# More expert groups made ahead, scatter-adds in eights between the row gathers, and row dots inside two top-k passes

## The chip, the cores and the metric

The kernel runs on one core of a Trainium2 chip. The metric is the device time of one execution in microseconds (us). The core has five engines with a fixed instruction order each: TensorE (PE, matmuls), VectorE (DVE), ScalarE (ACT), GpSimd (POOL) and SyncE (SP, which only issues DMAs). Each executes its own list in order and waits, where needed, for semaphores of the others or of DMAs. The lists are fixed when the kernel is built.

## The reference

The model is a two-layer trunk over 512 tokens of width 1024 in float32. Each layer is a mixer (pooling and retention, or a gated recurrence), then PEER, a layer of 16,384 single-row experts of which every token uses 8 heads x 16. PEER is where the change lies:

```python
q = (xt @ w_q).reshape(T, HEADS, 2, 128)
s = einsum('thpd,hpkd->thpk', q, sub_keys)          # 8 heads x 2 halves x 128 keys
s_top, i_top = top_k(s, 16)
cand = s_top[:, :, 0, :, None] + s_top[:, :, 1, None, :]
best, pos = top_k(cand.reshape(T, HEADS, 256), 16)
eid = take_along_axis(cand_id, pos); gate = softmax(best)
act = gelu(einsum('td,thkd->thk', xt, u_tab[eid]))
out = einsum('thk,thkd->td', gate * act, v_tab[eid])
```

A residual with layer norm follows each half.

## The kernel before

Tokens stand in four blocks (tb) of 128. Experts stand in 128 blocks of 128, four blocks to a group, 32 groups. Matmuls in float32 are made from three products of parts: a weight piece of 128 x 1024 is loaded by SP (`stream`, L173), ACT casts its high half `hi` (L169), DVE subtracts to get the low half `lo` (L170), and PE runs hi x hi, lo x hi and hi x lo (L185 to L187).

Most tokens use the experts densely: `mm1` makes the activations of one expert block for 352 tokens (24 matmuls of 352 columns), and the expert stage multiplies them by gates and by v. Block 3's 128 tokens gather their rows one by one in the expert stage (L968 to L993). The first 32 tokens of block 0 take a third way, the class `Scatter`: `place` (L79) gathers their u rows (POOL, L741), `dots` (L105, DVE) forms their dot products, `weigh` applies the Gelu (ACT, L111) and multiplies it into the gates (DVE, L113), and `add` (L127, POOL) adds the gates of block 0 to a table `gz` in HBM by indirect DMAs, 16 to a head, 128 to a layer. A head's adds wait until all of the previous head have landed.

The order in one PEER layer is as follows.

1. `route_topk`, four chunks c. A chunk projects a quarter of wq on PE (`proj_T`, 96 matmuls of 512 columns, which need four weight pieces, called a to d below). For each token block the keys are multiplied (L851) and DVE takes the top 16 of four key rows (L860 to L864). For block 0, `choose` then selects the experts of the chunk's two heads and `place` issues eight gathers of u rows into four buffers, `urow` and `urow3`. So the fifth gather needs the first four dots done. Before the change, dots stand behind token blocks 2 and 3, four each, then weigh, and the adds of a head stand behind it or behind the next chunk's choose. The next chunk's projection runs on PE while DVE still works on token blocks 2 and 3, and its weight halves are subtracted on DVE among the top-k.
2. `choose` for token blocks 3, 1 and 2, with PE transposes (L834).
3. `route_gates`, eight slices of 32 tokens, each in quarters: DVE makes one-hot tiles `oh`, `og` (L900, L901), PE multiplies them (L910, L911), ACT writes `gbuf` (L912), SP writes the slice to `gd` in HBM (L916).
4. `experts`: the expert blocks in turn, with 18 matmuls of 512 columns each (L1096), reading gates back from gd and gz.

Steps 1 to 3 leave PE room, so `lookahead` (L757) makes activations ahead: `NLA` groups of four mm1 blocks. They are placed by credits: the generators of steps 1 to 3 yield a cost at certain points, and each 2.8 credits puts one mm1 block there. What is left is made behind the last gate slice. The groups made ahead are written to HBM (`sp`, 704 KB a group) and read back in step 4, but for the last two (`KEEP`). The other groups' mm1 blocks are made in step 4, four blocks ahead of their use.

Of the kernel before, what the change touches and what calls it, by code (L numbers as in the profile page):

```python
# [15 lines left out]
ALU = mybir.AluOpType  # L16
# [16 lines left out]
NU = 32  # L33
TN = TD - NU
US = NU // 32
QN = P // NU
QC = 32 // QN
GQ = 8
LAG = GQ + 4
NSD = TD // 32  # L40
NLA = 19
NSZ = 4
KEEP = 2
ROT = 3
RAW = 5
QS = 8
Y2 = 1.85
YC = (1.5, 3.0, 3.0, 4.0)
AHEAD = 4
TAIL = 4  # L50
# [5 lines left out]
LANDED = mybir.DependencyInfo(mybir.DependencyClass.Sync, mybir.DependencyReason.DATA)  # L56


class Scatter:


    def __init__(self, k, pool, layer):
        nc, self.tc = k.nc, k.tc
        self.name = "gz%d" % layer
        self.layer = layer
        self.last = []
        self.todo = []
        self.gate = [k.pe.tile([P, 2, 16], F32, name="gate0", tag="gate0", bufs=4) for _ in range(4)]
        self.idx = [k.pe.tile([P, 2 * 16], I32, name="idx0", tag="idx0", bufs=4) for _ in range(4)]
        self.pcol = pool.tile([P, 1], F32, name="pcol", tag="pcol")  # L70
        nc.sync.dma_start(out=self.pcol, in_=k.io["pcol"])
        self.dst = k.dram.tile([NG, P, NSZ, NB, 32], F32, name=self.name, tag=self.name)
        z = pool.tile([P, NSZ * NB * 32], F32, name="zero", tag="zero")
        nc.gpsimd.memset(z, 0.0)
        for g in range(NG):
            nc.sync.dma_start(out=self.dst[g].rearrange("p s b t -> p (s b t)"), in_=z)

    def place(self, k, pool, c, k0, k1):
        nc = k.nc  # L79
        idx = self.idx[c]  # L80
        x = pool.tile([P, P], F32, name="ix0", tag="fi")[:, :32]
        y = pool.tile([P, P], F32, name="iy0", tag="fj")[:, :32]
        e = pool.tile([P, 32], I32, name="eu", tag="eu")
        ids = pool.tile([P, QC], I32, name="ids", tag="ids", bufs=2)
        nc.vector.scalar_tensor_tensor(e[:NU], k0[:NU], 128.0, k1[:NU], ALU.mult, ALU.add)
        for q in range(QN):
            nc.scalar.copy(ids[q * NU:(q + 1) * NU], e[:NU, q * QC:(q + 1) * QC])  # L87
        self.rows = []
        for j in range(QC):
            r, self.fetch = k.urow(pool, self.layer, ids, j)  # L90
            self.rows.append((j, r))
# [15 lines left out]
    def weigh(self, k, pool):  # L107
        nc = k.nc
        act = pool.tile([P, 32], F32, name="actu", tag="actu")
        for q in range(QN):  # L110
            nc.scalar.activation(act[:NU, q * QC:(q + 1) * QC], self.av[q * NU:(q + 1) * NU], AF.Gelu)  # L111
        gate = self.gate[self.chunk].rearrange("p h s -> p (h s)")
        nc.vector.tensor_tensor(gate[:NU], gate[:NU], act[:NU], ALU.mult)  # L113
        self.todo += [self.chunk * 2, self.chunk * 2 + 1]

    def add(self, k, n=1):
        nc, tc = k.nc, k.tc
        flat = self.dst.rearrange("g p s b (t o) -> (g p s b t) o", o=1)
        for _ in range(min(n, len(self.todo))):
            hd = self.todo.pop(0)  # L120
            c, h = divmod(hd, 2)
            gate = self.gate[c].rearrange("p h s -> p (h s)")
            key = "%s.%d" % (self.name, hd)
            head = []
            with tc.issue_after(self.fetch):
                for j in range(h * 16, h * 16 + 16):
                    d = nc.gpsimd.indirect_dma_start(  # L127
                        out=flat, out_offset=bass.IndirectOffsetOnAxis(ap=self.idx[c][:, j:j + 1], axis=0),
                        in_=gate[:, j:j + 1], in_offset=None, compute_op=ALU.add).ins
                    for p in self.last:  # L130
                        tc.add_manual_dep(d, p.name, LANDED, reason="adds of different heads may meet")
                    tc.declare_no_dep(d, group=key, reason="a head's sixteen experts differ")
                    tc.add_to_no_dep_group(key, d)
                    head.append(d)
            self.last = head

    def read(self, engine, out, g):
        d = engine.dma_start(out=out, in_=self.dst[g]).ins
        for p in self.last:
            self.tc.add_manual_dep(d, p.name, LANDED, reason="all adds of the last head")  # L140


class Kern:
# [623 lines left out]
    def route_topk(self, layer, xT, kT, gz):  # L767
        nc, tc, io = self.nc, self.tc, self.io
        with tc.tile_pool(name="rt", bufs=1) as rt, tc.tile_pool(name="rt2", bufs=2) as rt2, \
# [14 lines left out]
            def choose(tb, h0, n):  # L784
# [14 lines left out]
                for h in range(n):  # L799
                    c2 = rs2.tile([P, 64], F32, name="c2", tag="c2")  # L800
                    cv = cand[:, h, :]
                    nc.vector.max(out=best[:, h, 0:8], in_=cv)
                    nc.vector.max_index(out=pos[:, h, 0:8], in_max=best[:, h, 0:8], in_values=cv)
                    nc.vector.match_replace(out=c2, in_to_replace=best[:, h, 0:8], in_values=cv, imm_value=NEG)
                    nc.vector.max(out=best[:, h, 8:16], in_=c2)
                    nc.vector.max_index(out=pos[:, h, 8:16], in_max=best[:, h, 8:16], in_values=c2)
                    yield 0.7
                if tb == 3:
                    gate = self.gate3.rearrange("p (h s) -> p h s", h=8)
                elif tb == 0:  # L810
                    gate = gz.gate[h0 // 2]
# [30 lines left out]
            for c in range(4):  # L842
# [4 lines left out]
                for tb in range(NTB):  # L847
# [4 lines left out]
                                         start=True, stop=True)  # L852
                    ixs = rs2.tile([P, 4, 16], U32, name="ix", tag="ix", bufs=2)
                    for i in range(4):
                        hp = c * 4 + i
                        sc = ps[:, i * P:(i + 1) * P]
                        mx = stop[:, tb, hp, :]
# [371 lines left out]
```

## Time and profile before

| | |
|---|---|
| Median of three runs | 2801.23 us (2800.25 to 2803.93) |
| The profiled execution's own time | 2803.68 us |
| Its span on the core | 2801.9 us |
| Busy time of PE, DVE, POOL, ACT | 2745.8, 2359.3, 1352.6, 1116.5 us |
| Bytes moved | 788.34 MB |
| POOL adds (L127) | 256, 486.2 us busy |
| POOL gathers of u rows (L741) | 64, 86.9 us busy |

A row of a timeline reads: start in us, duration in us, engine, line, operation, output tile <- input tiles, shape, and in brackets the time the engine had idled before, with what ended that idle. A row of the waits reads: engine, tile and line that waited, engine, tile and line waited for, total us, times, longest. In the windows, PE busy etc. are us with the number of instructions, PEclk is the granted clock of TensorE as a share of full speed, DMA the busy share of its engines. "ACT ch" is a cast gate product ahead of an expert matmul, "DVE ka" and "kb" are tiles of the choose stage.

### The profile page before, as it was taken

What the parts mean: (1) busy time and instruction counts of PE and PEld (TensorE: products, weight loads), DVE (VectorE), ACT (ScalarE), POOL (GpSimd) and SP (SyncE); (2) the same over time, 40 slices, a digit from 0 to 9 for tenths busy, and PEclk for the clock granted to TensorE, in tenths of its full rate; (3) what the DMA queues carried; (4) which work ended last, traced back from release to release, by engine and by line L of the source; (5) the groups of instructions that cost most, each with busy time, mean ns of one, the idle gap of its engine ahead of it and who ended that gap; (6) DMA issues with size and microseconds to landing.
All of it is one profiled execution on the core that took longest, in us unless ns stands there. A gap on an engine that the chain in (4) does not pass through costs nothing.

```text
span 2801.9 us, 41670 instructions
## 1 busy us (share of the span) xinstructions
PE 2745.8 (98%) x15314; PEld 2449.4 (87%) x15314; DVE 2359.3 (84%) x4556; ACT 1116.5 (40%) x1575; POOL 1352.6 (48%) x865
## 2 busy tenths in 40 slices
PE   9999999999999999999999999999989999999998
PEld 7899899988888888888788898999978888888886
DVE  6678989867898989888798677899868888988887
ACT  3353336543333333333334343445543333333332
POOL 0006667864565666553000017667764556555651
PEclk9999999999999999999999999999999999999999
DMA  6357776999999999998222557686999999999993
GB/s 228 127 178 227 236 221 178 248 270 366 382 386 382 390 377 396 374 383 295 95 83 72 203 177 203 194 245 177 277 308 361 378 398 368 389 388 382 384 383 146
DMA packets 318318, 788.34 MB, mean 281 GB/s; under 512 B 62113, under 2 KB 128161, under 8 KB 318113
## 3 DMA queue, kind: packets, MB, share of 16 engines
q1 hardware_dynamic: 175808, 410.75, 41.4%
q0 software_dynamic: 120128, 303.22, 32.0%
q10 hardware_dynamic: 22176, 71.71, 6.4%
q8 instruction: 120, 1.97, 0.3%
q14 instruction: 86, 0.70, 0.1%
HBM read 708.50 MB, written 77.07 MB: 280 GB/s over the span
## 4 chain that ended last, share of the span: by engine, by line
PE 86%; DVE 7%; DMA 3%; POOL 2%; issue 1%; ACT 1%; SPq 0%; DVEq 0%; POOLq 0%; ACTq 0%
PE pB L1096 18%; PE pC L1096 18%; PE pA L187 12%; PE pA L185 12%; PE pA L186 12%; PE pC L185 2%; PE pC L186 2%; PE pC L187 2%; POOL gz L127 2%; DMA urow<-in_u,ids 2%; DVE lo L170 1%; PE pB L910 1%; DMA gd<-gbuf 1%; PE pB L911 1%; PE pB L851 1%
## 5 line engine op out<-in xcount | busy, mean ns | idle before, releaser
L169 ACT CAST hi<-raw 128x1024 fp32r<-128x1024 f32 (+1 forms) x609 | 637.8, 1050 | 962.9 <-PE pC L1096 368.2
L170 DVE TENSOR_TENSOR lo<-raw,hi 128x1024 fp32r<-128x1024 f32 (+1 forms) x609 | 733.7, 1215 | 184.5 <-ACT hi L169 156.4
L187 PE MATMUL pA<-xThi,lo 128*128 128x352 f32 (+2 forms) x1872 | 628.7, 336 | 11.2 <-DVE lo L170 11.2
L185 PE MATMUL pA<-xThi,hi 128*128 128x352 f32 (+2 forms) x1872 | 631.2, 337 | 0.6 <-ACT hi L169 0.3
L968 POOL DMA_INDIRECT row<-in_u,eid x256 | 407.3, 1591 | 464.4 <-DVE av L980 369.2
L186 PE MATMUL pA<-xTlo,hi 128*128 128x352 f32 (+2 forms) x1872 | 627.4, 335 | 0.6 <-DVE xTlo L170 0.6
L127 POOL DMA_INDIRECT gz<-gate,idx x256 | 486.2, 1899 | 130.6 <-issue 84.2
L968 POOL DMA_INDIRECT row<-in_v,eid x256 | 361.9, 1414 | 145.1 <-issue 58.5
L187 PEld LDWEIGHTS pA<-xThi,lo 128*128 128x128 f32 x1872 | 353.7, 189 | 28.6 <-DVE lo L170 14.1
L185 PEld LDWEIGHTS pA<-xThi,hi 128*128 128x128 f32 x1872 | 354.0, 189 | 18.3 <-ACT hi L169 1.2
L186 PEld LDWEIGHTS pA<-xTlo,hi 128*128 128x128 f32 x1872 | 353.9, 189 | 17.3 <-DVE xTlo L170 1.2
L993 DVE SCALAR_TENSOR_TENSOR h<-row,cf,h 128x1024 f32<-128x1024 f32 x256 | 329.4, 1287 | 6.7 <-DMA row<-in_v,eid 6.4
L980 DVE CUSTOM_DVE_ANT_0 row<-row,x 128x1024 f32<-128x1024 f32 x256 | 311.6, 1219 | 10.0 <-DMA row<-in_u,eid 9.7
L1096 PE MATMUL pB<-hi,ch 128*128 128x512 f32 x768 | 300.2, 391 | 17.9 <-DMA raw<-in_peer_ut 9.7
L1096 PE MATMUL pC<-hi,ch 128*128 128x512 f32 x768 | 299.9, 390 | 0.0
L1096 PE MATMUL pC<-lo,ch 128*128 128x512 f32 x768 | 299.6, 390 | 0.0
L1096 PE MATMUL pB<-hi,cl 128*128 128x512 f32 x768 | 299.6, 390 | 0.0
L1096 PE MATMUL pB<-lo,ch 128*128 128x512 f32 x768 | 299.5, 390 | 0.0
L1096 PE MATMUL pC<-hi,cl 128*128 128x512 f32 x768 | 299.3, 390 | 0.0
L170 DVE TENSOR_TENSOR cl<-gt,ch 128x768 fp32r<-128x768 f32 x128 | 122.0, 953 | 117.0 <-ACT ch L169 117.0
L741 POOL DMA_INDIRECT urow<-in_u,ids x64 | 86.9, 1358 | 273.4 <-ACT ids L87 203.7
L169 ACT CAST ch<-gt 128x768 fp32r<-128x768 f32 x128 | 107.2, 837 | 249.4 <-PE pC L1096 152.2
(280 smaller groups left out, 4541.9 us busy)
## 6 DMA issues: line engine op xcount, KB each, us to landing
raw<-in_peer_ut SPq DMA_DIRECT2D x256, 512.0 KB
raw<-in_peer_v SPq DMA_DIRECT2D x256, 512.0 KB
gd<-gbuf SPq DMA_DIRECT2D x16, 2048.0 KB
gt<-gd ACTq DMA_DIRECT2D x60, 512.0 KB
sp<-ge SPq DMA_DIRECT2D x34, 704.0 KB
ge<-sp ACTq DMA_DIRECT2D x34, 704.0 KB
raw<-in_peer_w_q SPq DMA_DIRECT2D x32, 512.0 KB
gz<-zero SPq DMA_DIRECT2D x64, 256.0 KB
```

What stands on the lines that cost most here:

```text
L127: d = nc.gpsimd.indirect_dma_start(out=flat, out_offset=bass.IndirectOffsetOnAxis(ap=self.idx[c][:, j:j + 1], axis=0), in_=gate[:, j:j + 1 ...
L169: self.nc.scalar.copy(hi, src)
L170: return self.nc.vector.tensor_tensor(lo, src, hi.bitcast(F32), ALU.subtract)
L185: nc.tensor.matmul(ps, ah, bh, start=(first and i == 0), stop=False)
L186: nc.tensor.matmul(ps, ah, bl, start=False, stop=False)
L187: nc.tensor.matmul(ps, al, bh, start=False, stop=(last and i == n - 1))
L741: d = self.nc.gpsimd.indirect_dma_start(out=t, out_offset=None, in_=self.io["u%d" % layer], in_offset=bass.IndirectOffsetOnAxis(ap=ids[:, ...
L851: nc.tensor.matmul(ps[:, i * P:(i + 1) * P], qs[i][:, ts], keys[:, i, :], start=True, stop=True)
L968: nc.gpsimd.indirect_dma_start(out=t, out_offset=None, in_=io[name], in_offset=bass.IndirectOffsetOnAxis(ap=at, axis=0))
L980: dot = nc.vector.tensor_tensor_reduce(ur, ur, x, 1.0, 0.0, ALU.mult, ALU.add, av[:, k:k + 1])
L993: nc.vector.scalar_tensor_tensor(acc, vr, c, acc, ALU.mult, ALU.add)
L1096: nc.tensor.matmul(acc[hf], a[:, ts], b[:, hf * 512:(hf + 1) * 512], start=first and i == 0, stop=last and i == 2)
```

## The change

Four things change; the arithmetic stays.

- `NLA` is 21 instead of 19: 84 mm1 blocks a layer are made ahead instead of 76.
- Costs: `Y2` is 1.6 instead of 1.85, so that each of the 16 yields of the gate stage gives 3.2 credits instead of 3.7; a head's yield in `choose` for token blocks other than 0 gives 1.2 instead of 0.7 (24 of them).
- Dots: instead of behind the top-k of token blocks 2 and 3, each four stand in the middle of it, ahead of the third key row (`DOTS`), behind a yield of 5.2 in place of 1.3 x 4.
- Adds: single adds are counted, not heads. `place` issues four gathers, eight adds that are still to do, four gathers, eight adds. The 16 adds behind chunk 0 and the rest behind chunk 3 (64) stand as before. A gather is issued after the last add made so far.

```diff
-NLA = 19
+NLA = 21
+DOTS = ((2, 2), (3, 2)) if NU == 32 else ...
-Y2 = 1.85
+Y2 = 1.6
 ...
         for j in range(QC):
-            r, self.fetch = k.urow(pool, self.layer, ids, j)
+            with ExitStack() as after:
+                if self.made:
+                    after.enter_context(tc.issue_after(self.made[-1]))
+                r, self.fetch = k.urow(pool, self.layer, ids, j)
             self.rows.append((j, r))
+            if j % 4 == 3:
+                self.add(k, 64 // QC)
 ...
-        self.todo += [self.chunk * 2, self.chunk * 2 + 1]
+        self.todo += [(self.chunk, j) for j in range(32)]
 ...
-    def add(self, k, n=1):
+    def add(self, k, n):
-        for _ in range(min(n, len(self.todo))):
-            hd = self.todo.pop(0)
-            c, h = divmod(hd, 2)
+        for c, j in self.todo[:n]:
+            if j % 16 == 0:
+                self.last, self.made = self.made, []
 ...
-                    yield 0.7
+                    yield 0.7 if tb == 0 else 1.2
 ...
                     for i in range(4):
+                        if (tb, i) in DOTS and gz.rows:
+                            yield 5.2
+                            with tc.issue_after(top.ins):
+                                gz.dots(self, 4)
 ...
                     if tb == 0:
                         yield from choose(0, c * 2, 2)
-                        if c:
-                            gz.add(self)
-                    else:
-                        n = (0, 1, 1)[tb - 1] * QC // 2
-                        yield 1.3 * n
-                        with tc.issue_after(top.ins):
-                            gz.dots(self, n)
-                gz.weigh(self, rs2)
-                if c == 0:
-                    gz.add(self)
-            gz.add(self, 8)
+                if DOTS[-1][0]:
+                    gz.weigh(self, rs2)
+                    if c == 0:
+                        gz.add(self, 16)
 ...
+            gz.add(self, 128)
```

The order on three engines shows what the build makes of it, in layer 0. First POOL in chunk 1 of the top-k, from its first gather on; `urow` are the gathered rows, `gz0` the adds, with the 16 adds of head 0 just ahead. Before:

```order
L741 DMA urow_2482<-in_u0,ids_2476 128x1024
L741 DMA urow_2484<-in_u0,ids_2476 128x1024
L741 DMA urow_2486<-in_u0,ids_2476 128x1024
L741 DMA urow3_2488<-in_u0,ids_2476 128x1024
L741 DMA urow_2490<-in_u0,ids_2476 128x1024
L741 DMA urow_2492<-in_u0,ids_2476 128x1024
L741 DMA urow_2494<-in_u0,ids_2476 128x1024
L741 DMA urow3_2496<-in_u0,ids_2476 128x1024
L127 DMA gz0_1420<-gate0_1410,idx0_1414 2097152x1 x16
L741 DMA urow_3189<-in_u0,ids_3183 128x1024
```

and now:

```order
L745 DMA urow_2482<-in_u0,ids_2476 128x1024
L745 DMA urow_2484<-in_u0,ids_2476 128x1024
L745 DMA urow_2486<-in_u0,ids_2476 128x1024
L745 DMA urow3_2488<-in_u0,ids_2476 128x1024
L131 DMA gz0_1420<-gate0_1410,idx0_1414 2097152x1 x8
L745 DMA urow_2498<-in_u0,ids_2476 128x1024
L745 DMA urow_2500<-in_u0,ids_2476 128x1024
L745 DMA urow_2502<-in_u0,ids_2476 128x1024
L745 DMA urow3_2504<-in_u0,ids_2476 128x1024
L131 DMA gz0_1420<-gate0_1410,idx0_1414 2097152x1 x8
```

The second four gathers now stand behind eight of head 1's adds; before, no add stood between the two fours.

Second, DVE in the same chunk, at the end of token block 3's top-k. `lo_2878` is piece d of the projection that PE runs meanwhile (the other `lo` are of mm1 blocks), the rows of L105 (now L111) are the second four dots, and the row on `gate0` is weigh's multiply. Before, from piece d to the first of the second four dots:

```order
L170 TENSOR_TENSOR lo_2878<-raw_2875,hi_2877 128x1024
L862 MATCH_REPLACE s2_2735<-stop_1471,pB_2717 128x128
L860 MAX stop_1471<-pB_2717 128x8
L863 MAX stop_1471<-s2_2735 128x8
L861 MAX_INDEX ix_2722<-stop_1471,pB_2717 128x8
L864 MAX_INDEX ix_2722<-stop_1471,s2_2735 128x8
L170 TENSOR_TENSOR lo_3024<-raw_3021,hi_3023 128x1024
L862 MATCH_REPLACE s2_2741<-stop_1471,pB_2717 128x128
L170 TENSOR_TENSOR lo_3069<-raw_3066,hi_3068 128x1024
L863 MAX stop_1471<-s2_2741 128x8
L864 MAX_INDEX ix_2722<-stop_1471,s2_2741 128x8
L105 ISA urow_2490,avu_2498<-urow_2490,xx_1402 128x1024
```

and now, from the third of those dots to piece d:

```order
L111 ISA urow_2502,avu_2514<-urow_2502,xx_1402 128x1024
L111 ISA avu_2514 128x1
L111 ISA urow3_2504,avu_2514<-urow3_2504,xx_1402 128x1024
L111 ISA avu_2514 128x1
L872 MATCH_REPLACE s2_2803<-stop_1471,pB_2717 128x128
L870 MAX stop_1471<-pB_2717 128x8
L873 MAX stop_1471<-s2_2803 128x8
L871 MAX_INDEX ix_2722<-stop_1471,pB_2717 128x8
L874 MAX_INDEX ix_2722<-stop_1471,s2_2803 128x8
L119 TENSOR_TENSOR gate0_1411<-gate0_1411,actu_2849 32x32
L174 TENSOR_TENSOR lo_2878<-raw_2875,hi_2877 128x1024
```

Piece d stood ahead of the second four dots and now stands behind them and behind weigh. The pieces a to c stand ahead of them in both.

Third, ACT between the last gate slice and the first expert product of layer 0. `ge` is the output of one mm1 block, `gbuf` of gate matmuls, `ch` the cast product. Before, from the last gate slice on:

```order
L912 ACTIVATE gbuf_6643<-pC_6730 128x128x4
L754 ACTIVATE ge_6760<-pA_6773 128x352
L169 CAST hi_6980<-raw_6978 128x1024
L754 ACTIVATE ge_6760<-pA_6805 128x352
L169 CAST hi_7037<-raw_7035 128x1024
L754 ACTIVATE ge_6760<-pA_6837 128x352
L169 CAST hi_7043<-raw_7041 128x1024
L754 ACTIVATE ge_6760<-pA_6869 128x352
L1030 DMA gt_6895<-gd0_1024 128x1024
L138 DMA gt_6895<-gz0_1420 128x512
L169 CAST ch_6899<-gt_6761 128x768
```

and now, up to the first of the casts `ch`; the last row on `gbuf` stands six rows ahead of the first row shown, with the evictions of two blocks between:

```order
L758 ACTIVATE ge_6874<-pC_6913 128x352
L173 CAST hi_7125<-raw_7123 128x1024
L142 DMA gt_7155<-gz0_1420 128x512
L173 CAST hi_7165<-raw_7163 128x1024
L758 ACTIVATE ge_6874<-pA_6945 128x352
L173 CAST hi_7178<-raw_7176 128x1024
L758 ACTIVATE ge_6874<-pC_6977 128x352
L173 CAST hi_7231<-raw_7229 128x1024
L758 ACTIVATE ge_7020<-pA_7033 128x352
L173 CAST hi_7240<-raw_7238 128x1024
L758 ACTIVATE ge_7020<-pA_7065 128x352
L173 CAST ch_7159<-gt_7021 128x768
```

The mm1 blocks between the last gate matmuls and the first expert matmul, each with a row on `ge`, were three and a part and are now nine. On PE the order of projections, keys and mm1 blocks through the top-k is the same but for a few neighbours; behind the last key there are 19 mm1 blocks instead of 16 ahead of the first transposes of `choose` and 9 instead of 7 ahead of the second.

More of the change, by code (lines that the diff above doesn't have):

```diff
@@ L37 @@
 QC = 32 // QN
+DOTS = ((2, 2), (3, 2)) if NU == 32 else ((2, 1), (3, 0), (3, 3), (0, 2))
 GQ = 8
@@ L66, in __init__ @@
         self.last = []
-        self.todo = []
+        self.todo, self.rows, self.made = [], [], []
         self.gate = [k.pe.tile([P, 2, 16], F32, name="gate0", tag="gate0", bufs=4) for _ in range(4)]
@@ L78, in place @@
     def place(self, k, pool, c, k0, k1):
-        nc = k.nc
+        nc, tc = k.nc, k.tc
         idx = self.idx[c]
@@ L113, in weigh @@
         nc.vector.tensor_tensor(gate[:NU], gate[:NU], act[:NU], ALU.mult)
-        self.todo += [self.chunk * 2, self.chunk * 2 + 1]
-    def add(self, k, n=1):
+        self.todo += [(self.chunk, j) for j in range(32)]
+    def add(self, k, n):
         nc, tc = k.nc, k.tc
         flat = self.dst.rearrange("g p s b (t o) -> (g p s b t) o", o=1)
-        for _ in range(min(n, len(self.todo))):
-            hd = self.todo.pop(0)
-            c, h = divmod(hd, 2)
+        for c, j in self.todo[:n]:
+            if j % 16 == 0:
+                self.last, self.made = self.made, []
+            key = "%s.%d" % (self.name, c * 2 + j // 16)
             gate = self.gate[c].rearrange("p h s -> p (h s)")
-            key = "%s.%d" % (self.name, hd)
-            head = []
             with tc.issue_after(self.fetch):
[L126 to L135, printed above, removed]
+                d = nc.gpsimd.indirect_dma_start(
+                    out=flat, out_offset=bass.IndirectOffsetOnAxis(ap=self.idx[c][:, j:j + 1], axis=0),
+                    in_=gate[:, j:j + 1], in_offset=None, compute_op=ALU.add).ins
+            for p in self.last:
+                tc.add_manual_dep(d, p.name, LANDED, reason="adds of different heads may meet")
+            tc.declare_no_dep(d, group=key, reason="a head's sixteen experts differ")
+            tc.add_to_no_dep_group(key, d)
+            self.made.append(d)
+        del self.todo[:n]
     def read(self, engine, out, g):
         d = engine.dma_start(out=out, in_=self.dst[g]).ins
-        for p in self.last:
+        for p in self.made:
             self.tc.add_manual_dep(d, p.name, LANDED, reason="all adds of the last head")
@@ L854, in route_topk @@
                     for i in range(4):
+                        if (tb, i) in DOTS and gz.rows:
+                            yield 5.2
+                            with tc.issue_after(top.ins):
+                                gz.dots(self, 4)
+                            if c and (tb, i) == DOTS[-1] and tb == 0:
+                                gz.weigh(self, rs2)
                         hp = c * 4 + i
@@ L868, in route_topk @@
                         yield from choose(0, c * 2, 2)
-                        if c:
-                            gz.add(self)
-                    else:
-                        n = (0, 1, 1)[tb - 1] * QC // 2
-                        yield 1.3 * n
-                        with tc.issue_after(top.ins):
-                            gz.dots(self, n)
+                if DOTS[-1][0]:
+                    gz.weigh(self, rs2)
+                    if c == 0:
+                        gz.add(self, 16)
+            if not DOTS[-1][0]:
+                gz.dots(self, 4)
                 gz.weigh(self, rs2)
-                if c == 0:
-                    gz.add(self)
-            gz.add(self, 8)
+            gz.add(self, 128)
             for tb in (3, 1, 2):
```

## The prediction

> **What bounds the kernel now.** I read the page first: the span, the engines' busy shares, the chain that ended last and the groups.
>
> ```profile
> span 2801.9 us, 41670 instructions
> ...
> PE 2745.8 (98%) x15314; PEld 2449.4 (87%) x15314; DVE 2359.3 (84%) x4556; ACT 1116.5 (40%) x1575; POOL 1352.6 (48%) x865
> ...
> PE 86%; DVE 7%; DMA 3%; POOL 2%; issue 1%; ACT 1%; SPq 0%; DVEq 0%; POOLq 0%; ACTq 0%
> ...
> L127 POOL DMA_INDIRECT gz<-gate,idx x256 | 486.2, 1899 | 130.6 <-issue 84.2
> ```
>
> TensorE (PE) is busy 98% of the span and carries 86% of the chain. PE executes in a fixed order, and the change adds and removes no matmul, so it can gain only what PE idles or runs at half clock, and lose only by new idle time. The page puts VectorE (DVE) at 7% of the chain and GpSimd (POOL) at 2%. One POOL add (L127) has a mean of 1,899 ns.
>
> The waits of PE over the whole run say where it idles:
>
> ```profile
> PE pA L187 <- DVE lo L170: 11.2, 7, 3.3
> PE pB L1096 <- DMA raw<-in_peer_ut: 9.7, 1, 9.7
> PE pB L1096 <- ACT ch L169: 8.2, 2, 7.4
> PE pC L834 <- DVE ka L954: 3.4, 1, 3.4
> PE pC L834 <- issue: 3.3, 1, 3.3
> ```
>
> The first row belongs to the top-k stage (a weight's low half is late), the second and third to the first expert matmuls of layers 1 and 0, the last two to the transposes of the choose stage in layers 1 and 0.
>
> The windows give clock and DMA load at these places; the columns are named in the header:
>
> ```profile
> core 0: us, PE busy (x) PEld busy (x) DVE busy (x) ACT busy (x) POOL busy (x), PEclk, DMA share, GB/s
> 349.00:370.90 21.90, 21.90 (x99) 18.13 (x98) 12.19 (x36) 7.21 (x13) 18.55 (x12) 1.00 0.53 133
> 471.00:477.90 6.90, 6.20 (x22) 6.20 (x23) 6.90 (x34) 0.85 (x3) 5.87 (x4) 0.51 0.60 102
> 624.00:643.00 19.00, 10.82 (x42) 8.36 (x42) 10.31 (x14) 4.13 (x5) 12.71 (x12) 0.82 1.03 415
> 660.00:1300.00 640.00, 640.00 (x3169) 560.91 (x3168) 562.67 (x644) 230.98 (x279) 361.96 (x238) 1.00 0.98 379
> 840.00:860.00 20.00, 20.00 (x105) 17.95 (x104) 15.13 (x17) 7.29 (x10) 9.29 (x6) 1.00 1.03 419
> 1733.90:1740.80 6.90, 5.85 (x14) 4.63 (x15) 6.90 (x22) 0.59 (x1) 6.29 (x3) 0.51 0.97 318
> 2071.00:2086.00 15.00, 5.26 (x16) 4.02 (x15) 4.89 (x6) 2.24 (x3) 8.06 (x9) 0.66 0.97 380
> ```
>
> The first row is one projection of a wq chunk at full rate: 96 matmuls in 21.9 us, 0.228 us each. Rows with PEclk 0.51 are half-clock spells; one of 6.90 us costs 3.4 us of work. In the expert stage (660 to 1300) PE is busy all the time.
>
> **Chunk 1 of the top-k: the new cost.** While chunk 1's scores are sorted, PE runs the projection of the next chunk; 25 matmuls into it PE needs the fourth low half, "d" (L170). These are the first matmul, the first that uses d, and the last:
>
> ```profile
> 281.54 0.39 PE L185 MATMUL pA<-xThi,hi 128*128 128x512 f32 x1
> ...
> 289.85 0.50 PE L187 MATMUL pA<-xThi,lo 128*128 128x512 f32 x1 [0.67 <-DVE lo L170]
> ...
> 306.98 0.40 PE L187 MATMUL pA<-xThi,lo 128*128 128x512 f32 x1
> ```
>
> On DVE, the first and last of the first four dots (L105), d, and the multiply of weigh (L113) behind the second four:
>
> ```profile
> 280.17 1.23 DVE L105 CUSTOM_DVE_ANT_0 urow<-urow,xx 128x1024 f32<-128x1024 f32 x1 [6.88 <-DMA urow<-in_u,ids]
> ...
> 283.93 1.23 DVE L105 CUSTOM_DVE_ANT_0 urow<-urow,xx 128x1024 f32<-128x1024 f32 x1
> ...
> 288.59 1.21 DVE L170 TENSOR_TENSOR lo<-raw,hi 128x1024 fp32r<-128x1024 f32 x1
> ...
> 299.72 0.18 DVE L113 TENSOR_TENSOR gate<-gate,actu 32x32 f32<-32x32 f32 x1 [0.93 <-ACT actu L111]
> ```
>
> POOL around it: the 16 adds of head 0, the first four gathers, and the fifth:
>
> ```profile
> 239.44 1.62 POOL L127 DMA_INDIRECT gz<-gate,idx  x1 [9.54 <-DVE gate L113]
> ...
> 269.18 2.01 POOL L127 DMA_INDIRECT gz<-gate,idx  x1 [0.30 <-issue]
> 271.50 1.47 POOL L741 DMA_INDIRECT urow<-in_u,ids  x1 [0.30 <-issue]
> ...
> 275.80 0.94 POOL L741 DMA_INDIRECT urow<-in_u,ids  x1 [0.30 <-issue]
> 281.67 1.80 POOL L741 DMA_INDIRECT urow<-in_u,ids  x1 [4.93 <-DVE itop L865]
> ```
>
> Before, d is subtracted at 288.59, ahead of the second four dots. The order of the changed kernel puts d behind those dots and behind weigh's multiply, and on POOL it puts eight adds between the first four gathers and the second four. So PE now waits for gathers that wait for adds. Step by step: the first four gathers end at 275.80 + 0.94 = 276.74. Sixteen adds took 271.50 - 239.44 = 32.06 us, 2.00 us each; eight take 16.0, so the second set starts at 276.74 + 0.30 + 16.0 = 293.0 (now 281.67). Its last gather is issued 4.3 later (275.80 - 271.50), at 297.3. Its dot starts 8.13 us after that issue, as 283.93 - 275.80 did, at 305.5, and ends at 306.7. Then 0.93 of idle for the Gelu, 0.18 for the multiply and 1.21 for d: 309.0. About 71 of the 96 matmuls are left: 71 x 0.228 = 16.2, to 325.2. PE will have idled some 20 us and resumes at half clock; between nothing and the 3.4 us of one spell I take 2.5: 327.7, against 306.98 + 0.40 = 307.4 before. The dots of chunk 0 now stand ahead of two or three subtracts, so weigh and the adds behind it start a little earlier; I take 1.5 off: **+18.8 us**.
>
> Layer 1 has the same order. Its first and last gather of that first set, and the last matmul of its projection:
>
> ```profile
> 1718.12 1.46 POOL L741 DMA_INDIRECT urow<-in_u,ids  x1 [0.30 <-issue]
> ...
> 1722.40 0.94 POOL L741 DMA_INDIRECT urow<-in_u,ids  x1 [0.30 <-issue]
> ```
>
> ```profile
> 1756.15 0.40 PE L187 MATMUL pA<-xThi,lo 128*128 128x512 f32 x1
> ```
>
> The second set starts at 1722.40 + 0.94 + 0.30 + 16.0 = 1739.6, its last dot at 1739.6 + 4.3 + 8.1 = 1752.0; d ends 1.23 + 0.93 + 0.18 + 1.21 later at 1755.6, the projection at 1755.6 + 16.2 + 2.5 = 1774.3, less 1.5, against 1756.55: **+16.2 us** (its own 3.3 us wait and half-clock spell are in the 1756.55 and are replaced). Bounds for each layer: adds at the first row's 1.62 us plus 0.30 of issue instead of 2.00 take 1 off, no half clock 2.5 more, a full spell adds 0.9; an add that must first see the previous head landed could add 2 to 4. So 12 to 23.
>
> **The other chunks.** In chunk 0 no adds stand between the gathers; d comes about 1.5 us later, which delays only work that is waiting for the adds anyway: nothing. In chunk 2 the eight adds delay the second set, but there the last low half of the projection stands ahead of the second dots, and what stands behind them is needed some 19 us later: nothing. In chunk 3 no projection follows. Its fourth and fifth gathers, and weigh's multiply:
>
> ```profile
> 394.05 0.94 POOL L741 DMA_INDIRECT urow<-in_u,ids  x1 [0.31 <-issue]
> 405.27 1.79 POOL L741 DMA_INDIRECT urow<-in_u,ids  x1 [10.28 <-DVE itop L865]
> ```
>
> ```profile
> 421.90 0.18 DVE L113 TENSOR_TENSOR gate<-gate,actu 32x32 f32<-32x32 f32 x1 [0.25 <-ACT actu L111]
> ```
>
> The fifth moves from 405.27 to 394.05 + 0.94 + 0.30 + 16.0 = 411.3, so DVE reaches the choose stage 6.0 us later than 421.90.
>
> **Choose.** There PE lost 3.3 us of idle and a spell of 3.4 us in layer 0, 3.4 of idle and about half a spell (1.7) in layer 1. The raised yields put three more blocks ahead of the first transposes and two more ahead of the second; a block is 24 matmuls, 624.13 - 620.33 = 3.80 us by the rows further down, so 11.4 us of cover is added first. Against it DVE is 6.0 late and has three more subtracts of 1.21: 9.6. That is even within 2 us, and I carry **0**, between -10 (3.3 + 3.4 + 3.4, clocks kept) and +8 (6.0 for layer 0 and 2 for layer 1 uncovered).
>
> By the rows, an idle of 3.3 us brings half clock. The Trainium skill, "TensorE: Matmul & The Clock Gate", section "Why this matters for your kernels", asks for no PE-idle gap above about 3 us, since one idle window halves the rate. By that rule, a choose stage whose idle is cut into pieces below 3 us keeps its clock, and the sum would be 5.1 (3.4 + 1.7) lower, 2812 us; I keep the spells, as the added blocks move the pieces and don't show how they split.
>
> **Gates.** Sixteen yields of 2 x 1.85 become 2 x 1.60: 8 credits, at 2.8 a block 2.9 blocks fewer beside the gate matmuls. The list of waits has no row of L910 or L911 on DVE, so there is slack now; if it is used up the loss is what DVE then lacks, at most 2.9 x 3.80 = 11. With nearly one block still beside each half slice I take **+1 a layer**, 0 to 5.
>
> **Front of the experts: the gain.** PE from the last gate matmul of layer 0 to the first expert matmul (L1096), and the write of the last gates on the chain:
>
> ```profile
> 612.64 0.41 PE L187 MATMUL pA<-xThi,lo 128*128 128x352 f32 x1
> ...
> 620.33 0.32 PE L187 MATMUL pA<-xThi,lo 128*128 128x352 f32 x1
> ...
> 624.13 0.32 PE L187 MATMUL pA<-xThi,lo 128*128 128x352 f32 x1
> 631.88 0.80 PE L1096 MATMUL pB<-hi,ch 128*128 128x512 f32 x1 [7.42 <-ACT ch L169]
> ```
>
> ```profile
> 613.58 9.28 DMA gd<-gbuf
> ```
>
> After the last gate matmul (612.64) stand three blocks and one matmul; then PE waits 7.42 us. The path under it, gate eviction, write (9.28 us), load, multiply, cast, takes 631.88 - 612.64 = 19.2 us. The order now puts nine blocks there: 9 x 3.80 = 34 us. In layer 1 the path is 3 x 3.80 + 9.7 = 21 us, also covered. So both idles go: in layer 0 8.2 us (19.00 - 10.82), plus about 1.5 of the half clock after it; in layer 1 9.7 (15.00 - 5.26), plus about 2.1. **-9.7 and -11.8**. ScalarE's queue now holds a load of gates two evictions behind the last gate slice, which waits for the 9.28 us write; the casts of the next five blocks stand ahead of it, so only evictions queue behind it: nothing. Late next would be the subtract of the first product, with 13 us to spare.
>
> **Experts.** Eight blocks leave this stage and are made ahead, so their PE time only moves. Two more groups are written out and read back, off PE's path as long as DMA keeps up.
>
> **Sum**: 18.8 + 16.2 + 0 + 2 - 9.7 - 11.8 = +15.5 us. The profiled execution's span is 2801.9 and its whole time 2803.68; the runs' median is 2801.23, so the steps, differences within that execution, are added to the median: **2817 us**. About 0.2%, 5.6 us, is what a measurement of this kernel can tell from no change.
>
> **Rivals.**
> A, faster: the stall at d is hidden or short and only the fronts' gain remains. Its place is the same, POOL's eight adds; it decides from 9 us per layer down ((21.5 - 2) / 2 = 9.7 breaks even). It needs adds of some 0.8 us, or PE work that fills the wait. For it: gathers issue in 0.94 us, so POOL can be that quick. Against: none of the quoted adds is under 1.6, their mean is 1.9, and the order of PE through the top-k is as before. With a stall of 0 to 3 it gives 2801.23 - 21.5 + 2 + 0 to 6: 2782 to 2788. Chance 0.12.
> B, slower still: the experts become bound by DMA. Per layer 2,304 expert matmuls x 0.228 = 525 us and 52 blocks x 3.80 = 198 make 723; without eight blocks 692. Bytes at 379 GB/s for 723 us are 274 MB, less eight weights of 0.52 MB and with two more reads of 0.70 MB: 271, or 392 GB/s. Against: 20 us moved 419. For: the DMA share is 0.98 already. At a ceiling of 379 / 0.98 = 387 the stage takes 700 instead of 692: +8 a layer, 2833. Chance 0.10. The Trainium skill, "DMA: Bandwidth & Descriptors", section "Where 436 GB/s comes from", says that the HBM side binds at about 358 GB/s; the measured 379 and 419 exceed that, and by it the stage would be bound already, which PE's 640.00 of 640.00 us denies.
> C, no change: waits of other kinds on the way (the adds start earlier than I think, the spells don't come), each stall about 10: 2797 to 2806. Chance 0.08.
> My forecast, stalls of 12 to 23 with the fronts gone: 2807 to 2830. Chance 0.70.
>
> **How the numbers follow.** The range leaves out A and the far end of B: 2798 to 2838. If the front gain failed instead, 15.5 + 21.5 gives 2838, its upper end. Faster by over 0.2%: A with a little of C, 0.13. Within: most of C and the low edge of the forecast, 0.10. Slower: 0.77.
>
> **What would show it.** Right: in both layers PE has one wait of 16 to 22 us on the subtract of L170 in the second projection, with the POOL row of eight adds in front of the fifth gather of that chunk; the expert matmul's waits of 9.7 and 7.4 are gone; no PE wait above 1 us between 660 and 1300. Wrong: d's wait under 9 us, adds under 1.2 us each, the front waits still there, or waits of the expert matmul on loads inside the stage.

## The result and the profile after

| | before | after |
|---|---|---|
| median | 2802.58 us (4 runs) | 2838.11 us (2836.68 to 2839.22, 4 runs) |
| span of the profiled execution | 2801.9 us | 2837.4 us |
| busy time of PE | 2745.8 us | 2756.7 us |

The changed kernel takes 1.0125 of the time before, with a 95% interval of 1.0107 to 1.0143: 35.5 us more. It is slower, as forecast, but by more than twice the forecast 15.5, and it lies just above the range (2798 to 2838).

The waits of PE in the changed kernel (engine, tile and line that waited, what for, total us, times, longest). L191 was L187, L174 was L170, L785 copies the projection's columns on ScalarE (ACT) and L117 is the Gelu of weigh:

```profile
PE pA L191 <- DVE lo L174: 44.5, 11, 13.8
PE pA L189 <- ACT actu L117: 5.2, 1, 5.2
PE pC L191 <- DVE lo L174: 5.0, 2, 2.5
PE pA L189 <- ACT qh L785: 4.6, 1, 4.6
```

The waits at the front of the experts (9.7 and 8.2 us before) are gone. The wait for a low half has grown from 11.2 us to 44.5, and the two larger waits on ACT are new.

Windows of the changed kernel: the projection beside chunk 1, six us of it, the projection beside chunk 2, a piece of choose, and the expert stage:

```profile
core 0: us, PE busy (x) PEld busy (x) DVE busy (x) ACT busy (x) POOL busy (x), PEclk, DMA share, GB/s
285.60:329.20 43.60, 26.78 (x99) 21.13 (x98) 22.10 (x67) 7.23 (x13) 25.76 (x16) 0.77 0.53 141
310.00:316.00 6.00, 6.00 (x14) 4.74 (x15) 3.13 (x7) 0.59 (x1) 5.32 (x3) 0.50 0.88 251
370.90:400.40 29.50, 24.25 (x100) 19.57 (x99) 13.43 (x35) 7.14 (x13) 20.40 (x14) 0.88 0.63 168
466.50:469.80 3.30, 3.30 (x13) 3.30 (x13) 3.30 (x8) 0.95 (x1) 2.88 (x2) 0.50 0.99 240
696.00:1340.00 644.00, 644.00 (x3130) 559.01 (x3129) 579.73 (x665) 231.64 (x277) 361.71 (x244) 1.00 0.99 388
```

The projection beside chunk 1 took 25.8 us before and takes 43.6, of which PE is busy 26.78, and from 310 to 316, right behind its long wait, the clock is 0.50; the one beside chunk 2 took 21.9 and takes 29.5. In the expert stage PE is busy 644.00 of 644.00 us, at 388 GB/s.

**Chunk 1, layer 0.** First POOL: the last of the first four gathers, and the first and last of the second four; the eight adds lie between.

```profile
275.54 0.94 POOL L745 DMA_INDIRECT urow<-in_u,ids  x1 [0.30 <-issue]
...
294.89 1.01 POOL L745 DMA_INDIRECT urow<-in_u,ids  x1 [0.30 <-issue]
...
298.72 0.94 POOL L745 DMA_INDIRECT urow<-in_u,ids  x1 [0.30 <-issue]
```

DVE: the first and the last of the second four dots, weigh's multiply and the subtract of piece d.

```profile
302.46 1.23 DVE L111 CUSTOM_DVE_ANT_0 urow<-urow,xx 128x1024 f32<-128x1024 f32 x1 [8.12 <-DMA urow<-in_u,ids]
...
306.30 1.23 DVE L111 CUSTOM_DVE_ANT_0 urow<-urow,xx 128x1024 f32<-128x1024 f32 x1
...
308.64 0.16 DVE L119 TENSOR_TENSOR gate<-gate,actu 32x32 f32<-32x32 f32 x1
308.73 1.21 DVE L174 TENSOR_TENSOR lo<-raw,hi 128x1024 fp32r<-128x1024 f32 x1
```

PE: the first matmul on the low half of piece a (the third of the projection), the one on d, and the first matmul behind the projection.

```profile
289.39 0.79 PE L191 MATMUL pA<-xThi,lo 128*128 128x512 f32 x1 [3.07 <-DVE lo L174]
...
309.99 0.80 PE L191 MATMUL pA<-xThi,lo 128*128 128x512 f32 x1 [13.75 <-DVE lo L174]
...
329.12 0.83 PE L855 MATMUL pB<-keys,qh 128*128 128x128 f32 x6
```

PE waits 13.75 us for d, which ends at 309.94, behind the dots, which wait 8.12 us for a gather that is issued at 294.89 because of the adds. In layer 1 it is the same:

```profile
1772.86 0.79 PE L191 MATMUL pA<-xThi,lo 128*128 128x512 f32 x1 [12.77 <-DVE lo L174]
```

**Chunk 2, layer 0.** On POOL, the last of the first four gathers and the first of the second four; the adds between took 374.27 - 354.82 = 19.5 us. Then DVE's last dot:

```profile
353.62 1.20 POOL L745 DMA_INDIRECT urow<-in_u,ids  x1 [0.30 <-issue]
...
374.27 1.01 POOL L745 DMA_INDIRECT urow<-in_u,ids  x1 [0.30 <-issue]
```

```profile
384.62 1.23 DVE L111 CUSTOM_DVE_ANT_0 urow<-urow,xx 128x1024 f32<-128x1024 f32 x1
```

ACT around it, in the changed kernel:

```profile
371.96 0.46 ACT L758 ACTIVATE ge<-pC 128x352 f32<-128x352 f32 x1
385.89 0.86 ACT L117 ACTIVATE actu<-avu 32x8 f32<-32x8 f32 x4 [13.47 <-DVE avu L111]
386.66 1.04 ACT L785 COPY qh<-pA 128x512 f32<-128x512 f32 x2
```

and the same place before, where the projection started at 349.05 instead of 370.96:

```profile
354.72 0.59 ACT L781 COPY qh<-pA 128x512 f32<-128x512 f32 x1 [4.21 <-PE pA L187]
358.38 0.86 ACT L111 ACTIVATE actu<-avu 32x8 f32<-32x8 f32 x4 [3.08 <-DVE avu L105]
360.16 0.59 ACT L781 COPY qh<-pA 128x512 f32<-128x512 f32 x1 [0.91 <-PE pA L187]
```

PE at the third group of columns:

```profile
387.27 0.79 PE L189 MATMUL pA<-xThi,hi 128*128 128x512 f32 x1 [5.25 <-ACT actu L117]
```

The projection has four groups of 24 matmuls, one to each 128 columns of wq, and two buffers `pA` for their results (in PSUM, where matmuls write), so the third group needs the first copied. Before, ACT copied the first group (354.72) and then did the Gelu. Now the Gelu stands ahead of the first copy in ACT's list, waits 13.47 us for the dots, and both copies wait behind it. PE stands still for 5.25 us and then runs at half clock for a while (0.88 over the window). In layer 1 the wait is 4.6 us.

### The profile page after: what moved, and what is told of

Read it like the earlier page. It is cut to its first block, busy times and chain, and to the rows that moved or that the text cites. A ratio compares the mean times of both kernels' runs of the same rounds, so it can differ in the third digit from the quotient of the medians.

```text
span 2837.4 us, 41674 instructions
## 1 busy us (share of the span) xinstructions
PE 2756.7 (97%) x15314; PEld 2456.2 (87%) x15314; DVE 2359.3 (83%) x4556; ACT 1116.1 (39%) x1575; POOL 1346.8 (47%) x865
## 5 line engine op out<-in xcount | busy, mean ns | idle before, releaser
L174 DVE TENSOR_TENSOR lo<-raw,hi 128x1024 fp32r<-128x1024 f32 (+1 forms) x609 | 731.4, 1217 | 193.9 <-ACT hi L173 174.5
L191 PE MATMUL pA<-xThi,lo 128*128 128x352 f32 (+2 forms) x1808 | 612.7, 339 | 44.5 <-DVE lo L174 44.5
L189 PE MATMUL pA<-xThi,hi 128*128 128x352 f32 (+2 forms) x1808 | 613.3, 339 | 11.9 <-ACT actu L117 5.2
L190 PE MATMUL pA<-xTlo,hi 128*128 128x352 f32 (+2 forms) x1808 | 610.5, 338 | 0.8 <-DVE xTlo L174 0.8
L131 POOL DMA_INDIRECT gz<-gate,idx x256 | 506.2, 1977 | 131.0 <-issue 76.1
L191 PEld LDWEIGHTS pA<-xThi,lo 128*128 128x128 f32 x1808 | 343.8, 190 | 64.9 <-DVE lo L174 49.1
L189 PEld LDWEIGHTS pA<-xThi,hi 128*128 128x128 f32 x1808 | 343.5, 190 | 30.4 <-ACT actu L117 5.7
L190 PEld LDWEIGHTS pA<-xTlo,hi 128*128 128x128 f32 x1808 | 343.4, 190 | 18.2 <-DVE xTlo L174 1.3
L191 PE MATMUL pC<-xThi,lo 128*128 128x352 f32 x672 | 217.6, 324 | 5.0 <-DVE lo L174 5.0
L189 PE MATMUL pC<-xThi,hi 128*128 128x352 f32 x672 | 219.9, 327 | 0.0
```

The source lines that it names most:

```text
L131: d = nc.gpsimd.indirect_dma_start(out=flat, out_offset=bass.IndirectOffsetOnAxis(ap=self.idx[c][:, j:j + 1], axis=0), in_=gate[:, j:j + 1 ...
L174: return self.nc.vector.tensor_tensor(lo, src, hi.bitcast(F32), ALU.subtract)
L189: nc.tensor.matmul(ps, ah, bh, start=(first and i == 0), stop=False)
L190: nc.tensor.matmul(ps, ah, bl, start=False, stop=False)
L191: nc.tensor.matmul(ps, al, bh, start=False, stop=(last and i == n - 1))
```

## The experiments

Times are medians; each ratio is to the kernel before on the same chip, with its 95% interval. The kernel before had medians of 2803.5 to 2805.4 there.

| run | what it is | us | ratio |
|---|---|---|---|
| ahead_only | before, the numbers alone | 2770.61 | 0.9873 [0.9857, 0.9890] |
| nla_only | before, 21 groups alone | 2782.88 | 0.9920 [0.9907, 0.9934] |
| rest_only | after, old numbers | 2870.39 | 1.0237 [1.0219, 1.0254] |
| dots_behind | after, dots back behind the top-k | 2796.06 | 0.9965 [0.9953, 0.9978] |
| adds16 | after, adds back behind all eight gathers | 2786.30 | 0.9933 [0.9917, 0.9950] |
| adds4 | after, four adds between the gathers | 2804.07 | 1.0004 [0.9995, 1.0014] |
| gelu_late | after, Gelu behind the copies | 2827.99 | 1.0082 [1.0065, 1.0099] |
| ahead_late | ahead_only, first 16 adds at the end | 2791.09 | 0.9964 [0.9950, 0.9978] |
| adds16_late | adds16, first 16 adds at the end | 2813.43 | 1.0038 [1.0026, 1.0051] |
| ahead_12 | ahead_only, 12 adds first, 20 behind | 2757.73 | 0.9834 [0.9820, 0.9847] |

The theory after the result was this: the new numbers only gain; the loss comes from second gathers that are late by eight adds, since two in-order lists put something of the projection behind the dots that need them, DVE piece d in chunk 1 and ACT the copies in chunk 2. The main rivals: the blocks made ahead cost something themselves, or only one of the two parts counts.

### The numbers alone: ahead_only

```diff
-NLA = 19
+NLA = 21
-Y2 = 1.85
+Y2 = 1.6
-                    yield 0.7
+                    yield 0.7 if tb == 0 else 1.2
```

(the rest as in the kernel before)

> The kernel before with the numbers alone: 21 groups ahead, 1.6 for the gate yields, 1.2 for the choose yields; dots and adds as before. Theory (the loss is all in dots and adds, the numbers only gain): both front waits gone (21.4 us), and DVE is not late at the choose stage, so up to 8 of its 14 go too: about 2778 (2770 to 2783). Rival (the numbers cost something themselves, in gates or by DMA in the experts): 2785 or above.

Measured 2770.61 us, 34 us less than before. The list of waits shows what is left; the longest is:

```profile
PE pA L187 <- DVE lo L170: 13.2, 8, 4.0
```

No wait of choose (L834) and none of the front is left in the list. PE's idle time in choose fell from 5.1 and 4.6 us to 0.9 and 0.2 in the two layers, so all but about 1 us of choose's loss went, not 8 of 14. The rival falls: the numbers cost nothing that shows.

### The groups alone: nla_only

```diff
-NLA = 19
+NLA = 21
```

> The kernel before with 21 groups instead of 19 and nothing else; the eight further blocks a layer all stand behind the last gate slice or where credits put them. Theory (the groups remove the front waits, the raised choose yields remove the waits of choose): fronts gone, choose idles as before: about 2782 (2778 to 2787). Rival (the groups do it all): 2772 or below.

Measured 2782.88 us, 22.5 less than before. The front waits are gone, and choose's are unchanged:

```profile
PE pC L834 <- DVE ka L954: 3.4, 1, 3.4
PE pC L834 <- issue: 3.3, 1, 3.3
```

So the groups bring the front (21.5 predicted, 22.5 measured), and the two other numbers bring choose, 12 us more. Rival rejected.

### The rest alone: rest_only

```diff
-NLA = 21
+NLA = 19
-Y2 = 1.6
+Y2 = 1.85
-                    yield 0.7 if tb == 0 else 1.2
+                    yield 0.7
```

> The changed kernel with the old numbers (19 groups, 1.85, 0.7): dots and adds alone. Theory (the parts add up, and the blocks made ahead cover DVE's lateness in choose): both front waits are back (21 us) and choose idles some 6 us more a layer: about 2870 (2862 to 2880). Rival (the loss comes from dots and adds together with the new numbers): 2850 or below.

Measured 2870.39 us, 66.9 more than before. The parts add up: 66.9 - 34.3 = 32.6, against 35.5 for the whole change.

```profile
PE pA L191 <- DVE lo L174: 46.0, 12, 13.4
PE pB L1103 <- ACT ch L173: 17.5, 3, 9.2
PE pA L189 <- ACT qh L785: 10.7, 2, 6.3
```

The front waits are back in the second row, and the waits for low halves and for the copies (third row) are close to those of the changed kernel (44.5 and 9.8).

### Which of the two parts: dots_behind and adds16

dots_behind takes the dots out of the top-k; eight adds stay between the gathers:

```diff
-                        if (tb, i) in DOTS and gz.rows:
-                            yield 5.2
-                            with tc.issue_after(top.ins):
-                                gz.dots(self, 4)
...
+                    else:
+                        n = (0, 1, 1)[tb - 1] * QC // 2
+                        yield 1.3 * n
+                        with tc.issue_after(top.ins):
+                            gz.dots(self, n)
```

> The changed kernel with the dots put back behind the top-k of token blocks 2 and 3; eight adds still stand between the gathers. The fourth low half is then ahead of the second dots, and the Gelu on ScalarE behind one copy of the projection. Theory (ScalarE's queue matters too): chunk 1 still stalls, since the fourth column group waits for the second copy, which stands behind the Gelu: waits of about 9 and 6 us there, none in chunk 2; about 2808. Rival (only the fourth low half behind the dots counts): no stall left, about 2788.

adds16 leaves the dots inside and puts the adds behind the eight gathers:

```diff
-            if j % 4 == 3:
-                self.add(k, 64 // QC)
...
                         yield from choose(0, c * 2, 2)
+                        if c:
+                            gz.add(self, 16)
```

> The changed kernel with the adds put back behind all eight gathers, sixteen at a time; dots stay inside the top-k. Theory: gathers come some 12 us earlier, the wait for the fourth low half in chunk 1 falls from 13.8 to about 10 us with the 3 of the piece ahead of it, ends about 8 and 7 us later than before; no wait in chunk 2: about 2806. Rival (the eight adds don't matter, the place of the dots does it alone): 2830 to 2838.

Measured 2796.06 and 2786.30 us, 12 and 20 below the expectations. Against the 2770.61 of the numbers alone, eights alone cost 25.5, dots inside alone 15.7, together 41.1; both at once cost 67.5 by the changed kernel's 2838.11 (66.9 by rest_only). The remaining 26 come only when both are there: late gathers, and the projection's pieces and copies behind the dots. By the lengths of the projections and choose's idle and half-clock time, some 14 of them are chunk 2, whose projection takes 22.0 us in both runs as in the kernel before, 5 are chunk 1 and 6 choose. Neither rival holds.

In dots_behind the wait comes where it was expected, smaller. ACT in chunk 1 copies the first group ahead of the Gelu and the second behind it, and PE waits at the fourth group:

```profile
292.98 0.59 ACT L785 COPY qh<-pA 128x512 f32<-128x512 f32 x1 [9.44 <-PE pA L191]
306.58 0.86 ACT L117 ACTIVATE actu<-avu 32x8 f32<-32x8 f32 x4 [13.02 <-DVE avu L111]
307.35 1.04 ACT L785 COPY qh<-pA 128x512 f32<-128x512 f32 x2
```

```profile
307.96 0.80 PE L189 MATMUL pA<-xThi,hi 128*128 128x512 f32 x1 [3.46 <-ACT qh L785]
```

3.46 us here and 4.29 in layer 1, where 9 and 6 were expected. In adds16, the wait for d in chunk 1 is 5.08 and 4.03 us instead of 13.75 and 12.77, and choose has no idle time; in dots_behind it has 4.1 and 4.2 us. My expectation had left choose as in the changed kernel; so it is the eight adds between the gathers that make DVE late there, by their place those of chunk 3.

### How many adds: adds4

```diff
             if j % 4 == 3:
-                self.add(k, 64 // QC)
+                self.add(k, 4 if j == 3 else 12)
```

> The changed kernel with four adds between the gathers of a chunk and twelve behind them, instead of eight and eight. Theory (the loss is the time of the adds, some 2 us each, ahead of the second gathers): chunk 1 ends about 8 us earlier in each layer, the wait in chunk 2 goes (14 us), and choose gets DVE 8 us earlier, worth some 12 in all: about 2796 (2788 to 2806). Rival (any add between costs the same, because it waits for the head before it to land): 2825 or above.

Measured 2804.07 us: 34 us of the 42 expected. The wait for d in chunk 1:

```profile
301.49 0.80 PE L191 MATMUL pA<-xThi,lo 128*128 128x512 f32 x1 [6.54 <-DVE lo L174]
```

It is 6.54 us plus 0.76 ahead of it, against 13.75, and 7.34 in layer 1, against 12.77: 5 to 7 us less for four adds fewer. The wait in chunk 2 fell to 1.7 and 2.6 us and did not go. With none (adds16), four and eight adds between the gathers the time is 2786.30, 2804.07 and 2838.11 us. The cost grows with the number of adds; a fixed price for having any adds there is rejected.

### The Gelu ahead of the copies: gelu_late

```diff
-                nc.scalar.copy(q, ps)
+                self.qcopy = nc.scalar.copy(q, ps)
...
                 self.proj_T(wq, c, xT, sink_q, early=c == 0)
+                if c > 1:
+                    with tc.issue_after(self.qcopy.ins):
+                        gz.weigh(self, rs2)
...
-                if DOTS[-1][0]:
+                if c in (0, 3):
                     gz.weigh(self, rs2)
```

> The changed kernel with weigh of chunks 1 and 2 behind the four copies of the next projection on ScalarE; adds and dots stay. Theory (the waits of 5.2 and 4.6 us in chunk 2, with the half clock after them, come from copies queued behind the Gelu): they go, 14 us, and one us a layer in chunk 1: about 2822. Rival (they come from the late dots on DVE or from the blocks made ahead): 2834 to 2838.

Measured 2827.99 us. ACT beside chunk 2:

```profile
373.73 0.58 ACT L785 COPY qh<-pA 128x512 f32<-128x512 f32 x1 [4.21 <-PE pA L191]
379.17 0.59 ACT L785 COPY qh<-pA 128x512 f32<-128x512 f32 x1 [4.86 <-PE pA L191]
384.61 0.59 ACT L785 COPY qh<-pA 128x512 f32<-128x512 f32 x1 [4.85 <-PE pA L191]
...
390.77 0.58 ACT L785 COPY qh<-pA 128x512 f32<-128x512 f32 x1
391.25 0.86 ACT L117 ACTIVATE actu<-avu 32x8 f32<-32x8 f32 x4
```

The copies now come when their groups end, every 5.4 us, the Gelu behind them, and the projection takes 22.0 us in both layers (368.06 to 390.02 in layer 0), as it did before the change: 7.4 and 6.5 us less than in the changed kernel. So the cause of this loss is shown. The total fell by 10 and not by 14, since choose in layer 0 lost 5 us more than in the changed kernel. A likely reason, not tested, is that PE now reaches choose earlier and DVE does not. ACT's list has a part in it: at 449.13 PE ends a wait of 2.13 us for an eviction of an mm1 block, and that eviction stands behind the Gelu of chunk 3, which waited 13.69 us.

### Early gathers: ahead_late, adds16_late and ahead_12

In ahead_only the waits left were mostly in chunk 1, where the gathers stand behind 16 adds. ahead_late moves these to the end:

```diff
                 gz.weigh(self, rs2)
-                if c == 0:
-                    gz.add(self)
```

> The numbers alone on the kernel before, and the 16 adds that stand ahead of chunk 1's gathers moved to the end, where 80 instead of 64 then stand. Theory: chunk 1's gathers start as soon as their rows are chosen, and its waits (4.1 and 4.5 us with 1.5 of half clock) go: about 2761 (2757 to 2766). Rival (the 80 adds end too late for the first load from the table and the front wait is back): 2772 or above.

Measured 2791.09: the rival. The waits in chunk 1 are gone (both projections take 22.0 us), but PE waits 14.8 and 13.1 us between the gates and the experts. On ACT there stands (ACTq is a DMA issued from ACT's list):

```profile
622.64 0.46 ACT L754 ACTIVATE ge<-pC 128x352 f32<-128x352 f32 x1 [2.68 <-PE pC L187]
...
646.82 0.33 ACTq L138 DMA_DIRECT2D gt<-gz  x1
647.18 1.04 ACT L169 CAST hi<-raw 128x1024 fp32r<-128x1024 f32 x1 [23.14 <-DMA gz<-gate,idx]
648.13 0.46 ACT L754 ACTIVATE ge<-pA 128x352 f32<-128x352 f32 x1
```

L138 loads a group from the table and waits until the last add has landed; ACT idles 23.14 us for it. The evictions of the mm1 blocks (L754) stand behind it, and none comes from 622.64 to 648.13. It is the same mechanism as in chunk 2.

adds16_late does the same to adds16 (the 16 adds for c == 0 left out there).

> The changed kernel with no add between a chunk's gathers and the first 16 adds moved to the end; dots stay inside the top-k. Theory (dots inside the top-k, ahead of the fourth low half and the Gelu ahead of the copies, cost only where gathers come late): chunk 1's waits go, about 2763 (2758 to 2772). Rival (the place of the dots costs by itself): 2780 or above.

Measured 2813.43. I had not counted the front, which waits again (30.0 us in both layers together). And the waits in chunk 1 stayed, although the gathers start at 263.3:

```profile
273.32 1.23 DVE L109 CUSTOM_DVE_ANT_0 urow<-urow,xx 128x1024 f32<-128x1024 f32 x1 [3.19 <-DMA urow<-in_u,ids]
...
276.84 1.23 DVE L109 CUSTOM_DVE_ANT_0 urow<-urow,xx 128x1024 f32<-128x1024 f32 x1 [2.28 <-DMA urow<-in_u,ids]
...
280.58 1.23 DVE L109 CUSTOM_DVE_ANT_0 urow<-urow,xx 128x1024 f32<-128x1024 f32 x1 [2.51 <-DMA urow<-in_u,ids]
```

```profile
297.09 0.80 PE L189 MATMUL pA<-xThi,lo 128*128 128x512 f32 x1 [5.09 <-DVE lo L172]
```

The first three waits are DVE's, for gathers, in front of the second to fourth dot. So the first dots, at the earlier place, come before their rows do even without adds, 8.0 us in all, and d is late by 5.09. That the place of the dots costs only with late gathers was wrong. In ahead_late the first gather starts at 264.46, the dots stand behind the top-k, and chunk 1's projections take 22.0 us; here they take 33.7 and 30.4, so the place of the dots by itself costs 11.7 and 8.5 us, waits and half clock together.

ahead_12 keeps the 64 adds at the end and makes 12 before chunk 1's gathers, as many as fit before the rows are chosen, and 20 behind them. It is built on dots_behind, with no adds in place:

```diff
-            if j % 4 == 3:
-                self.add(k, 64 // QC)
...
+                        if c:
+                            gz.add(self, 20 if c == 1 else 16)
...
                     if c == 0:
-                        gz.add(self, 16)
+                        gz.add(self, 12)
```

> The numbers alone on the kernel before, with 12 instead of 16 adds ahead of chunk 1's gathers, 20 behind them, 16 behind those of chunks 2 and 3, and 64 at the end as before. Theory (the waits in chunk 1 come from gathers that stand behind adds; only the number of adds at the end decides whether ScalarE's load from the table is late): chunk 1's waits and its half clock go, no front wait: about 2760 (2756 to 2765). Rival (the gathers are held by something else, or the front is at its limit already): 2768 or above.

Measured 2757.73 us, 1.7% below the kernel before and the best of all. The longest waits of PE that are left:

```profile
PE pA L189 <- DVE lo L172: 2.7, 3, 1.2
PE pC L254 <- DVE h L290: 2.2, 1, 2.2
```

PE is busy 2732.1 of a span of 2754.1 us.

## Why the prediction was wrong

The sign was right, and so was its main step; the sum left out a second stall. By its own steps, with sums over both layers:

| step | predicted | measured in the changed kernel |
|---|---|---|
| chunk 1, wait for d | +35.0 | +32.6 |
| front of the experts | -21.5 | -21.5 |
| chunk 2 | 0 | +14.0 |
| chunk 0 | 0 | +3.0 |
| choose, idle and half clock | 0 | +1.7 |
| gates | +2 | +0.3 |
| sum | +15.5 | +30.1 |

The measured terms are differences in the length of each projection (24.3 to 26.7 and 24.0 to 24.6 in chunk 0, 25.8 to 43.6 and 28.2 to 43.1 in chunk 1, 22.0 to 29.4 and 22.0 to 28.5 in chunk 2) and of idle and half-clock time in the other stages.

- **Chunk 1 was right in its mechanism; that its size came so near is in part luck.** In layer 0 the second gathers were forecast for 293.0 and start at 294.89, the last dot for 305.5 and 306.30, d's end for 309.0 and 309.94, the projection's end for 327.7, less 1.5, and about 329.1. Eight adds took 294.89 - 276.48 = 18.4 us, 2.3 each, where 2.0 was forecast. Of the 1.5 us that weigh was to bring forward, 0.2 reached the first gather (271.50 and 271.30). The wait was forecast as one of 16 to 22 us and was 13.75 and 12.77: PE came to d later, as the projection started at 285.69 instead of 281.54 and first waited 3.07 us for piece a. The half clock behind the waits was taken as 2.5 us a layer; by the clock and PE's busy time it cost 4.6 and 3.8. The two misses partly cancel. (25 matmuls stand ahead of d's first in the changed kernel, as the forecast counted; in the kernel before, whose rows it showed, there were 20.)
- **The step that failed is "what stands behind them is needed some 19 us later: nothing", for chunk 2.** It followed DVE's list only. Weigh also puts four Gelus on ACT, and ACT's list has the copies of the projection behind them; the third column group needs the first copy 10.9 us after its start, not 19. This was 7.4 and 6.5 us, and gelu_late shows it. The step on the front looked at just this question for ACT and answered it rightly; the step on the dots didn't ask it. The Trainium skill, "TensorE: Matmul & The Clock Gate", section "Architectural detail: the array is 16× 32×32, not 1× 128×128", says that the queues of ScalarE and VectorE are strictly first in, first out; the trace agrees, with copies standing behind a Gelu that waits 13.47 us.
- **Choose came out near zero, but as the difference of two larger terms.** Over both layers the numbers alone take away 13 of the 14 us that choose had lost; eights and dots inside cost some 15 again. The forecast set 11.4 us of cover against 9.6 of lateness a layer and took them as even, which holds; both are smaller than it had them.
- **The front and the gates** went as forecast. The eight blocks brought 21.5 us, and no wait of PE on loads showed in the expert stage at 388 GB/s, so rival B, with DMA as the bound, is out. Rivals A and C, with a short stall, are out by the 13.75 us.
- **Chunk 0** lost 2.4 us in layer 0 and 0.6 in layer 1: its dots, ahead of three of the pieces, make PE wait 0.47 and 2.04 us in layer 0, and a half-clock spell follows. I had counted d's lateness as hidden.
- **Half clock:** the forecast kept the spells in choose though its idle time might break up. It broke up, and a spell came all the same:

```profile
459.18 0.43 PE L191 MATMUL pA<-xThi,lo 128*128 128x352 f32 x1 [1.12 <-DVE lo L174]
...
465.73 0.43 PE L191 MATMUL pC<-xThi,lo 128*128 128x352 f32 x1 [2.48 <-DVE lo L174]
```

  After 1.12 and 2.48 us, the window of 466.50 to 469.80 above has PEclk 0.50. The Trainium skill, "TensorE: Matmul & The Clock Gate", section "Why this matters for your kernels", asks for no gap above about 3 us, and none was; the measurement decides. But the length of the pieces alone doesn't decide either: in choose of layer 1, pieces of 1.31, 1.11 and 2.48 us (the last ends at 1927.99) left the clock at 1.00 up to 1950, and only a piece of 2.71 us, which ends at 1949.96, was followed by 0.50, from 1951.3 to 1954.5. What does decide stays open.

Some 5 us of the 35.5 are not in the table. A half-clock spell of 3.4 us in the first 13 us of the profiled execution, 1.7 us of work, is one part. PE's idle time doesn't hold the rest: it grew by 24.6 us (from 56.1 to 80.7, span less busy time), and the idle parts of the terms above come to about as much. So some 3 us are busy time of PE that I could not place; their cause stays open.

## What to carry to other kernels

When work is moved to a later place, follow each of its instructions in the list of its own engine, and ask what is behind it there: here the dots on VectorE held a weight piece, and the Gelu on ScalarE held a copy that freed a PSUM buffer. Two moves that each cost little alone (15.7 and 25.5 us) can cost much more together (67.5), when one makes data late and the other puts needed work behind that data. A change of several parts is worth taking apart: the numbers alone gained 34 us, and the rest lost 67.

## What the runs showed of the hardware

- An indirect add of 128 single values, 512 bytes, holds GpSimd longer than a gather of 512 KB does: eight adds took 18.4 us in chunk 1, and four gathers 5.2 us (271.50 to 276.74 before).
- The clock of TensorE fell to half after idle pieces of 1.12 and 2.48 us some 6 us apart in choose of layer 0, none above 2.5; in layer 1 it stayed full after pieces of 1.31, 1.11 and 2.48 us.
- A load on ScalarE's queue that waits for a DMA holds the engine's own instructions behind it: ACT idled 23.14 us, with no eviction from 622.64 to 648.13, in ahead_late.
